# A hybrid decoder layer: the decode steps of its state-space heads in another place of the program, and dt by channel through DRAM

## The chip, the cores and the metric

One Trainium2 chip, one core. The metric is the device time of one execution in microseconds. The engines are named as in the profile: PE (TensorE: matmuls), DVE (VectorE), ACT (ScalarE), POOL (GpSimd), SP (SyncE, which here only issues transfers). Each engine works through its own instructions in an order fixed when the program is built.

## The reference

One layer for 1024 prompt positions and 8 decode rows (one new token each of 8 sequences), width 1024, all in f32:

```
proj = rmsnorm(x) @ w_in            # z (1536) | xBC (2048) | dt (24) | v (512)
xBC  = silu(causal_dwconv4(xBC));  dt = softplus(dt + bias);  a = -exp(a_log)
y    = ssd_scan(xs, dt, a, B, C, h0) + d_skip * xs      # 24 heads x 64, 4 groups of B and C, state 64, chunks of 128
y    = grouped_rmsnorm(y * silu(z)) # 4 groups of 384
x   += concat(y, pool_mixer(v)) @ w_out
x   += conv_ffn(rmsnorm(x));  out = rmsnorm(x)
```

For a decode row the scan is a single step on a state that is read from memory and written back: `h = exp(dt*a) * h0 + (dt*x) outer B`, `y = C . h + d_skip * x`. The pooling mixer subtracts the token from trailing means over 2 to 16 positions and maps each of four groups linearly. The outputs are y and all new states.

## The kernel before, in words

**Layout.** Channels lie on the 128 partitions, positions along a row: 1024 prompt columns and 8 decode columns. `win` is cut into 32 column tiles of 128: 0 to 11 are xs (12 tiles, two heads each), 12 and 13 are B and 14 and 15 are C of two halves, 16 to 27 are the gates z, 28 to 31 are v. Every f32 operand is split into a high part (an ACT copy to fp32r) and a low part (a subtraction); a product is three matmuls: high by high (L159), high by low (L160), low by high (L161), summed in PSUM in three pieces of 344 columns. Weights come in pieces of 128x512 by SP into `raw` (4 buffers, L130) and are split into `wop` (4 buffers): the high part on ACT (L140), the low part on `self.lo_eng` (L141), which is POOL for xs tiles 1 to 9 and DVE afterwards.

**Order of the program.** `startup` norms the input in three pieces (`norm`: L313 multiply, L319 high part, L329 low part, with a list `low` that delays the low parts by two multiplies) and computes tiles 12, 14 and 0. `dt_chain` turns dt to softplus, then makes running sums (`cum`, L422), their logarithms and exponentials, and writes the negated sums to DRAM (`acd`, L447). At its end it brings the decode rows' dt to a layout by channel: a transpose (L452), a copy, a masked multiply (L456), a select matmul (L461), `dtS`, and `dA = exp(-dt*exp(a_log))` (L470). `tables` chains ACT's table functions: each stands behind the one traced before it.

`ssd_phase` computes tiles 1 to 5; then tiles 13, 15, 6 to 9 with the first half's chunks between them (`ssd_tasks(0)`, taken from a queue by `between` at each piece of 344 columns); then tiles 10 and 11 with decode steps 0 to 2 between them; then gates 0 to 6 (tiles 16 to 22) with the second half's chunks, and decode steps 3 to 6 in four of these (L790). A `conv_tile` is convolved on ACT (L514) and DVE (three L516); its SiLU follows later.

**One chunk** of 128 positions has three functions. `decay` loads `mix` and `ce` from `acd`, shifts mix on DVE (L538), takes twelve exponentials of it and one of ce on ACT (L188) and multiplies ce by C on POOL (L553). `turn` transposes x and B on PE (L565, L574), copies them out (L575), masks C.B (L576), and multiplies (L578, L583). `apply` computes the chunk's state (L597, PSUM bank `pM`, of which there is one), the state's decay on POOL (L606) and sum on DVE (L610), and the output in bank `pY` (L620 from mix, L630 from ce), which L638 adds to xs.

**One decode step** (`sample_tile`, one of 12 tiles of xs) is POOL's: it loads the state (L666, 256 KB; every third tile, or at tile 7, also the rows of B and C, L662, that `sample_bc` wrote to DRAM after a transpose into `pM` and a copy), then does `dx`, `tmp = B*dx` (L671), `st = st*dA` (L672), their sum (L673), the store (L674), the product with C (L675), a tree of six additions (L680) and two small ones on xs (L681, L682). Its tags: `st`, `stt` and `bc` have one buffer each in the chunk stage; `sample_bc`'s small copy shares `stt`. Steps 7 to 11 stand in `project` beside gates 7 to 11, where the tags are shared with the pooling tiles (`v`, `mh`, `ml`, `vs`).

**A gate** (`gate_tile`) copies z out (L693), takes SiLU of all 1032 columns, multiplies the prompt columns of xs (L698) and the decode columns (L700); after every third, `group_norm` squares all 1056 columns (L710, L712, sums on POOL, L714, or on DVE for the last two groups) and `group_scale` sums over partitions by a matmul with ones (L721), takes Ln and Exp and scales prompt (L730) and decode columns (L730 again). Then come the four pooling tiles (`pool_tile`: v out of PSUM L847 and L849, pooling state by SP L843, first `memset` on POOL L842), `w_out`, and the ConvFFN, which takes the second half of the time.

The program is traced in this order, but the Tile framework places the instructions on each engine by a timeline of its own at build time: the program's order is a priority, and what is ready earlier by that timeline may go ahead. A tile whose tag has no free buffer waits until the older tile's last reader is done.

Of the kernel before, what the change touches and what calls it, by code (L numbers as in the profile page):

```python
# [10 lines left out]
F32 = mybir.dt.float32  # L11
# [59 lines left out]

M_ID, M_TRI, M_SEL, M_RM = 0, 128, 256, 384
NMAT = 384 + 12


class Kernel:
# [143 lines left out]
    def startup(self, first):  # L220
# [3 lines left out]
        with tc.tile_pool(name="start", bufs=1) as sp:  # L224
# [78 lines left out]
            def norm(c, ss, also=None):  # L303
# [6 lines left out]
                for k in range(KT):  # L310
# [10 lines left out]
                    if also is not None and k == 0:  # L321
                        with self.behind(act):
                            also()
                    while low and (len(low) > 2 or k == KT - 1):
                        j, xj = low.pop(0)
                        hi, lo = self.hn[j]
                        eng = nc.gpsimd if j == 2 or (j == 5 and c > 0) else nc.vector
                        with self.behind(prev if eng is nc.vector else None):
                            sub = eng.tensor_tensor(  # L329
                                out=lo[:, cols], in0=xj, in1=hi[:, cols].bitcast(F32), op=ALU.subtract  # L330
                            )
# [45 lines left out]
    def dt_chain(self, sp, dps):  # L377
# [34 lines left out]
        self.dt = self.const.tile([P, n9], F32, name="dt")  # L412
        nc.vector.scalar_tensor_tensor(out=self.dt, in0=t, scalar=0.0, in1=l, op0=ALU.max, op1=ALU.add)
        ea = cut(4 * n9, NH)
        self.tables(ea, self.c("alr", 0, NH), AF.Exp)
# [24 lines left out]
        for half in range(2):  # L440
# [12 lines left out]
        dts = cut(4 * n9 + NH, NB)  # L453
        nc.vector.tensor_copy(dts[:NH], tp[:NH, :NB])
        r = cut(900, XT * NB).rearrange("p (i b) -> p i b", b=NB)
        nc.vector.tensor_tensor(  # L456
            out=r[:NH], in0=self.mat[:NH, M_RM : M_RM + XT].unsqueeze(2).broadcast_to([NH, XT, NB]),
            in1=dts[:NH].unsqueeze(1).broadcast_to([NH, XT, NB]), op=ALU.mult,
        )
        tp = self.bank("pT")  # L460
        nc.tensor.matmul(  # L461
            tp[:, : XT * NB], self.mat[:NH, M_SEL : M_SEL + P], r[:NH].rearrange("h i b -> h (i b)"),
            start=True, stop=True,
        )
        self.dtS = self.const.tile([P, XT, NB], F32, name="dtS")
        nc.vector.tensor_copy(self.dtS.rearrange("p i b -> p (i b)"), tp[:, : XT * NB])
        ec = cut(1000, XT)
        self.tables(ec, self.c("alc", 0, XT), AF.Exp)
        self.dA = self.const.tile([P, XT, NB], F32, name="dA")
        nc.vector.scalar_tensor_tensor(  # L470
            out=self.dA, in0=self.dtS, scalar=-1.0, in1=ec.unsqueeze(2).broadcast_to([P, XT, NB]),
            op0=ALU.mult, op1=ALU.mult,
        )
        self.tables(self.dA, self.dA, AF.Exp)

# [177 lines left out]
    def sample_tile(self, q, i):  # L653
# [3 lines left out]
        mk = lambda s, shape: self.ph.tile(shape, F32, tag=self.tags[s][0], name=self.nm(s), bufs=self.tags[s][1])  # L657
        if i % 3 == 0 or i == 7:
            self.bc = mk("bc", [P, 2, NB, NST])
            for j in range(2):  # L660
                src = self.bcd[q : q + 1, :, j * P + g * NST : j * P + (g + 1) * NST]
                nc.gpsimd.dma_start(self.bc[:, j], src.rearrange("o b n -> (o b) n").partition_broadcast(P))  # L662
# [5 lines left out]
        tmp = mk("stt", [P, NB, NST])  # L668
        bcast = lambda a: a.unsqueeze(2).broadcast_to([P, NB, NST])
# [14 lines left out]
    def gate_tile(self, n, i, between):  # L684
# [10 lines left out]
        def gate():  # L695
            z = box[0]
            self.tables(z, z, AF.Silu)
            nc.vector.tensor_tensor(out=y[:, :SEQ], in0=y[:, :SEQ], in1=z[:, :SEQ], op=ALU.mult)  # L698
            ys = self.xs_samp(y)
            nc.vector.tensor_tensor(out=ys, in0=ys, in1=z[:, SEQ:TOK], op=ALU.mult)  # L700
            if i % 3 == 2:
                self.group_norm(i // 3)
# [4 lines left out]
    def group_norm(self, g):  # L707
        nc = self.nc
        sq = [self.short(SW, "sq") for _ in range(2)]
        nc.scalar.activation(sq[0], self.xs[3 * g], AF.Square)  # L710
        for i in range(1, 3):
            nc.scalar.activation(sq[1], self.xs[3 * g + i], AF.Square)  # L712
            eng = nc.gpsimd if g < 2 else nc.vector
# [3 lines left out]
    def group_scale(self, g, sq):  # L717
        nc = self.nc
        for j, (o, w) in enumerate(((0, 512), (512, 512), (1024, 32))):
            pb = self.bank(("pT", "pY")[j % 2])  # L720
# [3 lines left out]
        for i in range(3):  # L724
            y = self.xs[3 * g + i]
            for o, a, r in (
                (y[:, :SEQ], y[:, :SEQ], sq[1][:, :SEQ]),
                (y[:, SEQ:TOK], self.xs_samp(y), self.xs_samp(sq[1])),
            ):
                nc.vector.scalar_tensor_tensor(  # L730
                    out=o, in0=a, scalar=self.c("nw", 3 * g + i), in1=r, op0=ALU.mult, op1=ALU.mult
                )

    def project(self):

        nc, d, tc = self.nc, self.d, self.tc
        self.bcd = self.dram.tile([2, NB, 2 * P], F32, name="bcd")
        self.xs, self.bt, self.ctl = [None] * XT, {}, {}

        with ExitStack() as outer:  # L740
# [5 lines left out]
            with self.banks(g=4, pT=2, pY=1, pM=1) as self.ps, tc.tile_pool(name="mix", bufs=1) as self.ph:  # L746

                self.tags = {"bc": ("v", 2), "st": ("mh", 1), "stt": ("ml", 1), "dx": ("vs", 2)}
                for i in range(7, 12):
                    self.sample_tile(1, i)  # L750
                    self.gate_tile(16 + i, i, None)
                self.pool_groups()

    def ssd_phase(self):
# [19 lines left out]
        def ssd_tasks(q):  # L774
# [5 lines left out]
            def step(c):  # L780
# [18 lines left out]

        self.lo_eng = nc.gpsimd  # L800
        for n in range(1, 6):
            self.keep(n, self.conv_tile(n, n, None))
        ssd_tasks(0)
        credit[:] = 0.35, 0.6
        for n in (13, 15, 6, 7, 8, 9):
            self.keep(n, self.conv_tile(n, n, between))
        flush()
        self.lo_eng = nc.vector
        self.sample_bc(1)
        for i in range(3):  # L810
            queue.append(lambda i=i: sample(i))
        credit[1] = 0.7
# [698 lines left out]
def _mats():  # L1511
# [3 lines left out]
    m[:, M_TRI : M_TRI + P] = s <= t  # L1515
    m[:, M_SEL : M_SEL + P] = (s % 2) == (t // 64)
    m[:, M_RM : M_RM + XT] = (s // 2) == np.arange(XT)[None, :]
    return m
# [94 lines left out]
```

## Time and profile before

| | |
|---|---|
| median of 3 runs | 1408.72 us (1400.76 to 1411.55) |
| the profiled execution's own time | 1407.76 us |
| its span, first to last instruction | 1406.0 us |
| mean granted PE clock | 0.984 |
| chunk stage of the first half | about 117 to 220 us |
| chunk stage of the second half | about 269 to 390 us |
| gates 7 to 11 | about 397 to 465 us |
| bytes moved by DMA | 228.09 MB |

The page's first part gives each engine's busy time, share of the span and number of instructions. A row of the timeline reads: start, duration, engine, line, operation, output<-inputs, count; in brackets the idle time of that engine just before and what ended it. A row of the waits reads: who waited, for whom: us in total, times, the longest. A row of the stages reads: from:to, length, then busy us (and instructions) of PE, weight load, DVE, ACT and POOL, the granted PE clock, the share of the DMA engines and GB/s. A row of the groups reads: instruction and shape xcount | busy us, mean ns | idle before.

### The profile page before, as it was taken

Reading aid. Unit: us, or ns where it says so; the run is one execution under the profiler, and the core shown is the slowest. Engines: PE = TensorE matmul, PEld = TensorE weight load, DVE = VectorE, ACT = ScalarE, POOL = GpSimd, SP = SyncE. Lnnn points to the kernel's source line nnn. Section 1 sums busy time; section 2 is a strip of 40 time slices with the busy share of each in tenths; the row PEclk is TensorE's granted clock in tenths of the full one; section 3 lists DMA queues with packets and bytes.
Section 4 is the critical chain, followed back from the end, with each engine's and each line's share of the span. In section 5 each row is a group of like instructions: output and inputs, shape, how many; then the busy total and the mean of one; then the engine's idle time right before and its main releaser. Section 6 shows DMA issues by size and latency. Waiting matters only on the chain. (4 is left out here: it accounts for less than half of the span.)

```text
span 1406.0 us, 26779 instructions
## 1 busy us (share of the span) xinstructions
PE 1360.4 (97%) x10360; PEld 1312.9 (93%) x10360; DVE 991.2 (70%) x1453; ACT 700.6 (50%) x1408; POOL 561.5 (40%) x704
## 2 busy tenths in 40 slices
PE   8999999979999999999979999999999999999997
PEld 7799879968799999899979999999999999999997
DVE  6575898669865684844689877777776787567743
ACT  6346774546644451311456545554554465444452
POOL 4233465888668305774222212212222224214122
PEclk9999999989999999999999999999999999999999
DMA  6031235243331256675477877777777769657513
GB/s 248 1 108 38 93 118 168 81 142 116 94 104 62 74 192 209 214 253 178 152 204 148 210 205 193 187 207 183 185 187 201 196 207 328 225 185 235 180 55 121
DMA packets 117820, 228.09 MB, mean 162 GB/s; under 512 B 19884, under 2 KB 37116, under 8 KB 117692
## 3 DMA queue, kind: packets, MB, share of 16 engines
q1 hardware_dynamic: 73772, 130.21, 29.3%
q0 software_dynamic: 27056, 70.22, 19.8%
q10 hardware_dynamic: 16864, 25.95, 5.6%
q8 instruction: 81, 1.33, 0.4%
q14 instruction: 47, 0.39, 0.1%
HBM read 169.64 MB, written 45.15 MB: 153 GB/s over the span
## 5 line engine op out<-in xcount | busy, mean ns | idle before, releaser
L1118 PE MATMUL g<-op,wop 128*128 128x258 f32 x3696 | 446.9, 283 | 4.3 <-DVE op L1048 1.6
L1118 PEld LDWEIGHTS g<-op,wop 128*128 128x128 f32 x3696 | 445.3, 189 | 5.6 <-DVE op L1048 2.0
L140 ACT ACTIVATE wop<-raw 128x512 fp32r<-128x512 f32 (+1 forms) x208 | 125.9, 608 | 231.2 <-PE g L161 139.7
L1300 PE MATMUL g<-op,wop 128*128 128x258 f32 x1848 | 224.9, 283 | 1.6 <-ACT op L210 0.9
L159 PE MATMUL g<-hh,wop 128*128 128x344 f32 x696 | 226.1, 325 | 0.0
L160 PE MATMUL g<-hl,wop 128*128 128x344 f32 x696 | 225.3, 324 | 0.0
L1300 PEld LDWEIGHTS g<-op,wop 128*128 128x128 f32 x1848 | 222.5, 189 | 2.7 <-ACT op L210 1.1
L161 PE MATMUL g<-hh,wop 128*128 128x344 f32 x696 | 224.8, 323 | 0.0
L141 DVE TENSOR_TENSOR wop<-raw,wop 128x512 fp32r<-128x512 f32 (+1 forms) x186 | 159.7, 862 | 83.3 <-ACT wop L140 81.5
L140 ACT ACTIVATE wop<-s 128x512 fp32r<-128x512 f32 (+1 forms) x136 | 83.6, 620 | 137.6 <-PE g L1300 51.9
L1098 POOL DMA_DIRECT2D s<-s x44 | 37.7, 857 | 249.8 <-DVE wop L141 89.2
L159 PEld LDWEIGHTS g<-hh,wop 128*128 128x128 f32 x696 | 132.2, 190 | 1.2 <-issue 1.1
L161 PEld LDWEIGHTS g<-hh,wop 128*128 128x128 f32 x696 | 132.1, 190 | 1.2 <-issue 1.2
L160 PEld LDWEIGHTS g<-hl,wop 128*128 128x128 f32 x696 | 132.1, 190 | 0.5 <-issue 0.4
L1200 DVE SCALAR_TENSOR_TENSOR acc<-u,cst,acc 128x1048 f32<-128x1048 f32 x88 | 115.2, 1309 | 12.2 <-ACT acc L1198 10.6
L141 DVE TENSOR_TENSOR wop<-s,wop 128x512 fp32r<-128x512 f32 (+1 forms) x136 | 92.1, 682 | 36.5 <-ACT wop L140 34.1
L1178 DVE TENSOR_TENSOR u<-u,g 128x258 f32<-128x258 f32 (+2 forms) x176 | 58.0, 354 | 72.2 <-PE g L1118 67.6
L1175 ACT ACTIVATE u<-g 128x258 f32<-128x258 f32 (+2 forms) x220 | 69.6, 340 | 71.2 <-PE g L1118 71.2
L160 PE MATMUL g<-yl,wop 128*128 128x344 f32 x288 | 93.4, 325 | 3.2 <-DVE yl L211 3.2
L161 PE MATMUL g<-yh,wop 128*128 128x344 f32 x288 | 93.0, 323 | 0.0
L159 PE MATMUL g<-yh,wop 128*128 128x344 f32 x288 | 92.9, 323 | 0.0
L1270 POOL DMA_DIRECT2D g<-td x77 | 41.2, 539 | 123.1 <-DVE op L211 70.2
(276 smaller groups left out, 2333.9 us busy)
## 6 DMA issues: line engine op xcount, KB each, us to landing
s<-wup SPq DMA_DIRECT2D x88, 256.0 KB, 3.2
g<-td POOLq DMA_DIRECT2D x77, 258.0 KB, 4.5
raw<-wup SPq DMA_DIRECT2D x66, 256.0 KB, 4.1
raw<-win SPq DMA_DIRECT2D x58, 256.0 KB, 2.7
mix<-acd SPq DMA_DIRECT2D x16, 768.0 KB, 4.5
td<-acc ACTq DMA_DIRECT2D x22, 516.0 KB, 6.1
s<-wup POOLq DMA_DIRECT2D x44, 256.0 KB, 5.3
s<-s POOLq DMA_DIRECT2D x44, 256.0 KB, 3.9
```

The lines of the kernel that those rows point to most:

```text
L140: self.nc.scalar.activation(hi, raw[:, :w], AF.Copy)
L141: lo_eng.tensor_tensor(out=lo, in0=raw[:, :w], in1=hi.bitcast(F32), op=ALU.subtract)
L159: nc.tensor.matmul(ps[:, :n], wh, xh[:, sl], start=(first and k == 0), stop=False)
L160: nc.tensor.matmul(ps[:, :n], wh, xl[:, sl], start=False, stop=False)
L161: nc.tensor.matmul(ps[:, :n], wl, xh[:, sl], start=False, stop=(final and k == last))
L1098: nc.gpsimd.dma_start(t, raw[acc] if acc in raw else w[acc][j], accum_op=ALU.add)
L1118: nc.tensor.matmul(out, a, b, start=(p in OPENS and j == 1), stop=(j == 12), skip_group_check=True)
L1175: a = nc.scalar.activation(out, ps[:, s], AF.Copy, scale=-1.0 if p in ("p5", "p4") else 1.0)
L1178: nc.vector.tensor_tensor(out=out, in0=out, in1=ps[:, s], op=op)
L1200: nc.vector.scalar_tensor_tensor(out=acc, in0=u[:, k : k + FW], scalar=self.c("fw", 3 * n + k), in1=acc, op0=ALU.mult, op1=ALU.add)
L1270: self.loaded = self.nc.gpsimd.dma_start(st[:, j], self.td[i + j][ROW[p]]).ins
L1300: self.pe = nc.tensor.matmul(out, a, b, start=(s == 0 and i == 0 and j == 0), stop=(s == len(PIECES) - 1 and i == nk - 1 and j == 2),).ins
```

## The change

Seven things are changed together.

1. `dtS` and `dA` are made right behind `dt`: the decode rows' dt goes to DRAM (`dtd`, transposed by the access pattern) and back as two broadcasts over 64 partitions, all three issued by ACT. The transpose, mask and select matmul go, and two blocks of the constant `mat` with them.
2. `sample_bc(0)` and decode steps 0 to 4 stand behind conv tiles 1 to 5, step 5 behind tile 13; `sample_bc(1)` stands behind the first half's chunk 2.
3. Steps 6 to 8 stand beside gates 7 to 9, steps 9 to 11 behind gate 11. The rows of B and C (`bc`) share the tag `pf` (2 buffers); for steps 9 to 11 state and `tmp` share one tile of that tag.
4. The low parts of the weights of tiles 1 to 5 (and what is loaded ahead for them) go from POOL to DVE.
5. For gates 6 to 11, SiLU of the decode columns goes to a tile of its own (`zs`); their gate, and the group norm of groups 2 and 3, treat prompt columns alone.
6. `group_decode` gates and norms the decode columns of groups 2 and 3, behind pooling tiles 3 and 1.
7. In `norm` of the first piece, the low part is delayed by one multiply, not by two.

```diff
-                    while low and (len(low) > 2 or k == KT - 1):
+                    while low and (len(low) > min(c + 1, 2) or k == KT - 1):
...
         nc.vector.scalar_tensor_tensor(out=self.dt, in0=t, scalar=0.0, in1=l, op0=ALU.max, op1=ALU.add)
+
+        dtd = self.dram.tile([NH, NB], F32, name="dtd")
+        nc.scalar.dma_start(dtd.rearrange("h b -> b h"), self.dt[:NB, n8:n9])
+        self.dtS = self.const.tile([P, XT, NB], F32, name="dtS")
+        for g in range(2):
+            nc.scalar.dma_start(self.dtS[64 * g : 64 * g + 64], dtd[g::2].partition_broadcast(64))
+        ec = cut(1000, XT)
+        self.tables(ec, self.c("alc", 0, XT), AF.Exp)
+        self.dA = self.const.tile([P, XT, NB], F32, name="dA")
+        nc.vector.scalar_tensor_tensor(
+            out=self.dA, in0=self.dtS, scalar=-1.0, in1=ec.unsqueeze(2).broadcast_to([P, XT, NB]),
+            op0=ALU.mult, op1=ALU.mult,
+        )
+        self.tables(self.dA, self.dA, AF.Exp)
...
-        tp = self.bank("pM")
-        nc.tensor.transpose(tp[:NH, :NB], self.dt[:NB, n8:n9], self.mat[:NB, M_ID : M_ID + NB])
...
-        self.tables(self.dA, self.dA, AF.Exp)
...
-        if i % 3 == 0 or i == 7:
+        if i % 3 == 0:
...
-        st = mk("st", [P, NB, NST])
+        if self.tags["st"] is None:
+            pair = self.ph.tile([P, 2, NB, NST], F32, tag="pf", name=self.nm("st"), bufs=2)
+            st, tmp = pair[:, 0], pair[:, 1]
+        else:
+            st, tmp = mk("st", [P, NB, NST]), mk("stt", [P, NB, NST])
...
-            self.tables(z, z, AF.Silu)
+            if i < 6:
+                self.tables(z, z, AF.Silu)
+            else:
+                self.tables(z[:, :SEQ], z[:, :SEQ], AF.Silu)
+                self.tables(self.zs[:, i - 6], z[:, SEQ:TOK], AF.Silu)
...
+    def group_decode(self, g):
+
+        nc = self.nc
+        pb = self.bank("pT")
+        for i in range(3):
+            y, s = self.xs[3 * g + i], self.zs[:, 6 + i]
+            rows = y[:, SEQ:TOK]
+            nc.vector.tensor_tensor(out=rows, in0=self.xs_samp(y), in1=self.zs[:, 3 * g + i - 6], op=ALU.mult)
+            nc.vector.tensor_tensor(out=s, in0=rows, in1=rows, op=ALU.mult)
+            nc.tensor.matmul(pb[:, :NB], self.ones, s, start=(i == 0), stop=(i == 2))
+        r = self.zs[:, 9]
+        self.rsqrt(r, pb[:, :NB], 1.0 / 384.0)
+        for i in range(3):
+            rows = self.xs[3 * g + i][:, SEQ:TOK]
+            nc.vector.scalar_tensor_tensor(
+                out=rows, in0=rows, scalar=self.c("nw", 3 * g + i), in1=r, op0=ALU.mult, op1=ALU.mult
+            )
...
-                self.tags = {"bc": ("v", 2), "st": ("mh", 1), "stt": ("ml", 1), "dx": ("vs", 2)}
+                self.tags = {"bc": ("pf", 2), "st": ("mh", 1), "stt": ("ml", 1), "dx": ("vs", 2)}
                 for i in range(7, 12):
+                    if i < 10:
+                        self.sample_tile(1, i - 1)
+                    self.gate_tile(16 + i, i, None)
+                self.tags["st"] = None
+                for i in range(9, 12):
                     self.sample_tile(1, i)
-                    self.gate_tile(16 + i, i, None)
...
-                if c == -1 and q == 0:
-                    self.sample_bc(q)
-                if q == 1 and c in (0, 2, 4, 6):
-                    sample(3 + c // 2)
+                if (q, c) == (0, 2):
+                    self.sample_bc(1)
...
-        self.lo_eng = nc.gpsimd
         for n in range(1, 6):
             self.keep(n, self.conv_tile(n, n, None))
+            if n == 1:
+                self.sample_bc(0)
+            sample(n - 1)
         ssd_tasks(0)
         credit[:] = 0.35, 0.6
+        self.lo_eng = nc.gpsimd
         for n in (13, 15, 6, 7, 8, 9):
             self.keep(n, self.conv_tile(n, n, between))
+            if n == 13:
+                sample(5)
         flush()
         self.lo_eng = nc.vector
-        self.sample_bc(1)
-        for i in range(3):
-            queue.append(lambda i=i: sample(i))
...
             pf[g] = self.pool_tile(g, g == 0)
+            if g in (3, 1):
+                self.group_decode(2 if g == 3 else 3)
```

More of the change, by code (lines that the diff above doesn't have):

```diff
@@ L69 @@
 NCONST = _n
-M_ID, M_TRI, M_SEL, M_RM = 0, 128, 256, 384
-NMAT = 384 + 12
+M_ID, M_TRI = 0, 128
+NMAT = 256
 class Kernel:
@@ L449, in dt_chain @@
         )
-        tp = self.bank("pM")
-        nc.tensor.transpose(tp[:NH, :NB], self.dt[:NB, n8:n9], self.mat[:NB, M_ID : M_ID + NB])
[L453 to L473, printed above, removed]
-        self.tables(self.dA, self.dA, AF.Exp)
     def samp(self, t):
@@ L708, in group_norm @@
         nc = self.nc
-        sq = [self.short(SW, "sq") for _ in range(2)]
-        nc.scalar.activation(sq[0], self.xs[3 * g], AF.Square)
+        w = SW if g < 2 else SEQ
+        sq = [self.short(SW, "sq")[:, :w] for _ in range(2)]
+        nc.scalar.activation(sq[0], self.xs[3 * g][:, :w], AF.Square)
         for i in range(1, 3):
-            nc.scalar.activation(sq[1], self.xs[3 * g + i], AF.Square)
+            nc.scalar.activation(sq[1], self.xs[3 * g + i][:, :w], AF.Square)
             eng = nc.gpsimd if g < 2 else nc.vector
@@ L718, in group_scale @@
         nc = self.nc
-        for j, (o, w) in enumerate(((0, 512), (512, 512), (1024, 32))):
+        for j, (o, w) in enumerate(((0, 512), (512, 512), (1024, 32))[: 3 if g < 2 else 2]):
             pb = self.bank(("pT", "pY")[j % 2])
@@ L727, in group_scale @@
                 (y[:, :SEQ], y[:, :SEQ], sq[1][:, :SEQ]),
-                (y[:, SEQ:TOK], self.xs_samp(y), self.xs_samp(sq[1])),
-            ):
+                (y[:, SEQ:TOK], self.xs_samp(y), self.xs_samp(sq[1]) if g < 2 else None),
+            )[: 2 if g < 2 else 1]:
                 nc.vector.scalar_tensor_tensor(
@@ L738, in project @@
         self.xs, self.bt, self.ctl = [None] * XT, {}, {}
+        self.zs = self.const.tile([P, 10, NB], F32, name="zs")
         with ExitStack() as outer:
@@ L1515, in _mats @@
     m[:, M_TRI : M_TRI + P] = s <= t
-    m[:, M_SEL : M_SEL + P] = (s % 2) == (t // 64)
-    m[:, M_RM : M_RM + XT] = (s // 2) == np.arange(XT)[None, :]
     return m
```

6 lines of the change are left out of this document (3 added, 3 removed).

## The prediction

> **What bounds the kernel now.** The page was read first, then the waits of TensorE (PE), then busy time by stage, then engine timelines around the longest waits.
>
> ```profile
> span 1406.0 us, 26779 instructions
> PE 1360.4 (97%) x10360; PEld 1312.9 (93%) x10360; DVE 991.2 (70%) x1453; ACT 700.6 (50%) x1408; POOL 561.5 (40%) x704
> ```
> ```profile
> PE pY L630 <- POOL ce L553: 9.8, 2, 9.2
> PE pM L565 <- DVE h L610: 3.7, 4, 1.9
> PE g L160 <- DVE hl L329: 2.6, 2, 2.3
> PE pY L620 <- DVE mix L583: 2.9, 2, 2.1
> PE pT L571 <- DVE cb L576: 2.8, 1, 2.8
> ```
> ```profile
> 100.00:140.00 40.00, 40.00 (x257) 39.29 (x256) 22.88 (x24) 26.39 (x50) 15.67 (x19) 1.00 0.13 40
> 140.00:190.00 50.00, 46.80 (x401) 41.54 (x400) 44.93 (x59) 34.99 (x78) 26.56 (x21) 0.97 0.37 119
> 280.00:305.00 25.00, 15.81 (x107) 12.77 (x106) 14.11 (x26) 11.17 (x25) 18.98 (x27) 0.73 0.41 122
> 305.00:390.00 85.00, 78.69 (x627) 69.05 (x626) 76.32 (x100) 53.56 (x114) 67.27 (x60) 0.96 0.35 112
> 390.00:465.00 75.00, 75.00 (x497) 72.17 (x496) 41.50 (x48) 36.98 (x55) 57.34 (x73) 1.00 0.28 87
> 296.10:302.90 6.80, 6.80 (x43) 4.97 (x45) 2.33 (x7) 0.00 (x0) 6.15 (x11) 0.50 0.10 39
> 337.00:340.40 3.40, 3.40 (x14) 3.12 (x13) 3.40 (x2) 1.99 (x7) 2.48 (x2) 0.51 0.33 122
> 378.00:381.40 3.40, 3.39 (x21) 2.11 (x22) 3.40 (x3) 3.37 (x5) 3.17 (x2) 0.50 0.02 7
> ```
>
> PE is busy 97% of the span, so only its 45.6 idle us, and the stretches at half clock after some waits, can be won. A stage row reads: its length, then busy us (and instructions) of PE, weight load, DVE, ACT, POOL, then the granted clock. PE is idle 9.2 us in 280 to 305 and 6.3 us in 305 to 390: the second half's chunks, with decode steps on POOL beside them. The last three rows are half-clock stretches behind those waits: 6.8, 3.4 and 3.4 us at 0.50, half of each lost: 6.8 us. So this stage loses 9.2 + 6.3 + 6.8 = 22.3 us.
>
> Whether POOL's decode steps are the cause stands in three timelines, ACT, POOL, PE:
>
> ```profile
> 279.37 0.83 ACT L188 ACTIVATE ce<-ce 128x768 f32<-128x768 f32 x1
> 291.18 0.83 ACT L188 ACTIVATE ce<-ce 128x768 f32<-128x768 f32 x1
> ```
> ```profile
> 280.53 1.84 POOL L662 DMA_DIRECT2D bc<-bcd  x2
> ...
> 286.69 1.83 POOL L671 TENSOR_TENSOR stt<-bc,dx 128x512 f32<-128x512 f32 x1 [2.15 <-DMA bc<-bcd]
> ...
> 293.24 1.03 POOL L672 TENSOR_TENSOR st<-st,dA 128x512 f32<-128x512 f32 x1 [2.45 <-DMA st<-st_ssm]
> 294.24 1.79 POOL L553 TENSOR_TENSOR ce<-ce,xs 128x768 f32<-128x768 f32 x1
> ```
> ```profile
> 296.08 1.54 PE L630 MATMUL pY<-ce,h 64*64 64x128 f32 x12 [9.19 <-POOL ce L553]
> ...
> 310.40 0.87 PE L597 MATMUL pM<-xd,bT 128*64 128x384 f32 x4
> ```
>
> Chunk 1's ce left ACT at 280.2, but POOL, in order, had decode steps 2 and 3 ahead of the multiply, with waits for their transfers, and came to it at 294.24. PE had stood since 286.9. The smaller waits name DVE, yet POOL stands behind the 2.8 us one:
>
> ```profile
> 259.35 0.69 DVE L141 TENSOR_TENSOR wop<-raw,wop 128x512 fp32r<-128x512 f32 x1 [3.45 <-ACT wop L140]
> ```
> ```profile
> 330.13 5.25 DVE L141 TENSOR_TENSOR wop<-raw,wop 128x512 fp32r<-128x512 f32 x1
> 335.31 0.55 DVE L575 COPY xd<-pT 128x384 f32<-128x384 f32 x1
> ```
> ```profile
> 330.07 2.48 POOL L714 TENSOR_TENSOR sq<-sq,sq 128x1056 f32<-128x1056 f32 x1
> 332.50 1.04 POOL L671 TENSOR_TENSOR stt<-bc,dx 128x512 f32<-128x512 f32 x1
> ```
>
> The same subtraction takes 0.69 us alone and 5.25 us beside an unbroken run of POOL work; the copy that PE waits for starts behind it.
>
> **The change, part by part.**
>
> Decode steps 0 to 5 leave the chunks of the second half, 6 goes behind them. What stays there for POOL is ce, the state multiply h and the squares. I take 20 of the 22.3 us as won (bounds 12.6, the long wait with its half clock, and 22.3). What is late next: chunk 2, whose ce leaves ACT at 292.0 (second ACT row). PE began chunk 2 at 310.4, 14.3 us after the wait, 3.4 of them lost to the clock; without the wait it comes there at 286.9 + 10.9 = 297.8, later than 292.0, so the wait is not handed on at once.
>
> Where do steps 0 to 5 go? One step's price is read where POOL has little else:
>
> ```profile
> L674 POOL DMA_DIRECT2D ssm_s<-stt x5 | 3.0, 602 | 1.5 <-POOL stt L673 1.5
> L672 POOL TENSOR_TENSOR st<-st,dA 128x512 f32<-128x512 f32 x5 | 6.4, 1286 | 6.7 <-DMA st<-st_ssm 6.7
> ```
>
> Five steps ran there, one store each, for the 57.3 us of POOL in the row 390 to 465: 11.4 us of POOL each and, with the wait for st (6.7 over five) and small gaps, some 14 us from one to the next (an estimate). Their start hangs on SiLU of B and C, which today stands behind dA in ACT's order of tables:
>
> ```profile
> 109.95 0.28 ACT L188 ACTIVATE dA<-dA 128x96 f32<-128x96 f32 x1 [3.41 <-DVE dA L470]
> 110.24 1.28 ACT L181 ACT_TABLE_LOAD   x1
> 111.53 4.98 ACT L188 ACTIVATE xs<-xs 128x1056 f32<-128x1056 f32 x5
> ```
> ```profile
> 69.75 0.39 DVE L413 SCALAR_TENSOR_TENSOR dt<-dtw 128x216 f32<-128x216 f32 x1
> ```
> ```profile
> DMA to landing us min/median/max: 4.7/5.5/6.1
> ```
>
> dt is ready at 70.1. The route through DRAM is two transfers one after the other; by the bc loads (last row, 4.7 to 6.1 us) they are bounded at 12 us, so dA can be there by 82 instead of 110. SiLU follows by about 90, since the convolution's sums come first on DVE, and the B and C rows of step 0, through DRAM again, by about 102 (both estimates from these rows). The price of the route: exp of a_log, and with it the running sums and acd, now stand behind dA on ACT, up to 12 us later than now. The first chunk's POOL work was only due at 143 (row below), which covers it; without cover PE would stand up to those 12 us at the sums. Two issues on ACT also wait for the first landing, with PSUM copies of PE queued behind them; three banks cover that. I take 0.
> ```profile
> L456 DVE TENSOR_TENSOR dtw<-mat,dtw 24x96 f32<-24x96 f32 x1 | 1.3, 1337 | 0.0
> L730 DVE SCALAR_TENSOR_TENSOR xs<-xs,cst,sq 128x8 f32<-128x8 f32 x12 | 5.6, 467 | 0.0
> ```
>
> The dearest instruction of the removed select costs 1.3 us of DVE. The two decode norms put 18 eight-column instructions in place of 12: 2.8 us more of DVE at 0.47, beside the pooling tiles, whose matmuls cover it (without them, 2.8). Net 0.
>
> The lower halves of tiles 1 to 5, ten subtractions, move to DVE: 6.9 us at 0.69, in 70 us where (row 100 to 140) DVE is 57% busy. Hidden; at 5.25 each they would not be.
>
> From 102 to the first chunk's POOL work, three steps fit:
>
> ```profile
> 143.13 1.82 POOL L553 TENSOR_TENSOR ce<-ce,xs 128x768 f32<-128x768 f32 x1 [10.30 <-ACT ce L188]
> ```
>
> Three remain, 34 us of POOL, in a stage where DVE is 90% and POOL 53% busy (row 140 to 190). What a step beside chunks costs: 305 to 390 held steps 4 to 6 and lost 6.3 + 3.4 = 9.7 us, 3.2 each; over the whole stage 22.3 for five, 4.5 each. Three steps: 9.7 to 13.4, and 0 if the order leaves POOL's chunk work ahead. I take 8, under the nearest row, because the idle POOL of 100 to 140 may hold more than three. The small copy for the second half's B and C now waits for step 5 to free its buffer, holding the bank pM that the chunks use; that is within these 8.
>
> The Trainium skill's page "SBUF — State Buffer", section "Who interferes with whom", says that a DVE instruction with two SBUF inputs and a GpSimd one that reads SBUF exclude each other for the whole instruction. The 5.25 us row agrees. By it, the sum would be that of the third rival below, 1419, against 1397 by the stage rows.
>
> Startup: hl of the first tile comes ahead of the third multiply.
>
> ```profile
> 12.77 1.59 DVE L313 SCALAR_TENSOR_TENSOR x<-x,cst,rs 128x344 f32<-128x344 f32 x1
> ```
>
> So it starts 1.5 us sooner; PE's 2.3 us wait there shrinks, but hl of the next tile then follows its own multiply. I take 1 (0 to 3.2, the upper with the half clock gone: 3.4 us at 0.50).
>
> ```profile
> 16.20:19.60 3.40, 3.40 (x13) 3.25 (x13) 3.40 (x7) 2.13 (x6) 0.43 (x1) 0.50 1.06 376
> ```
>
> Late steps: beside the last gates POOL now has six steps instead of five, 11.4 to 14 us more, and steps 9 to 11 share one buffer. Queued behind: the loads of pooling state on SP wait for dx of steps 10 and 11, and the next tiles' weights stand behind them on SP; PE waits for those. Gates cover part of it. I take 2 us lost (0 to 14, one step).
>
> Sum against the profiled execution, 1407.76 us with 1406.0 of span: 1407.8 - 20 - 1 + 8 + 2 = 1396.8, say **1397**. The median of three runs was 1408.72, 1 us above it.
>
> **The rivals.**
>
> *Nothing comes back.* POOL's idle time of 100 to 140 (24 us) and of the chunk stage behind it (23 us) takes the steps, and the chunks' POOL work keeps its place: 1407.8 - 20 - 1 = 1387. For: those 47 us are most of the 68 that six steps need, and only the chunks after 190 meet the rest; against: the B and C rows may come later than 102.
>
> *The stall only changes its place.* Late steps: SP held for 12 us as steps 10 and 11 run late, PE starved as long, its half clock 3.4: 1407.8 - 21 + 8 + 12 + 3.4 = 1410. For: SP's order is fixed beforehand and both buffers' waits lie in it; against: PE has no idle time at all in 390 to 465.
>
> *DVE locked out in the first half's chunks: slower.* In 140 to 190 DVE has 5.1 us free. If each of the 34 POOL us of three steps keeps DVE out, DVE ends 29 us late there, and PE, which waits for its mix and xd, with it, plus 3.4 of clock: 1407.8 - 21 + 29 + 3.4 = 1419. It decides from 18 us of delay on. For: the 5.25 us row. Against: in 305 to 390 DVE and POOL were busy 143.6 us of 85 together, so most DVE work does run beside POOL.
>
> *It does not do what it says.* The waits stay since ACT's exps, not POOL, hold the chunks: 1407. Against: ce was ready 14 us ahead of its multiply.
>
> **How the numbers follow.** My forecast 0.40; nothing comes back 0.25; stall moved 0.14; DVE locked out 0.14; no effect 0.07. The forecast's own range is 1390 to 1404; below it the second case, which with all 22.3 and startup's 3.2 makes 1382; above it the third and the fourth: 1380 to 1419. One per cent is about what a measurement of this kernel can tell from no change; it lies at 1394.6 and 1422.8. Faster by more: nearly all of the second case and a third of mine, 0.39. Slower by more: most of the lock-out's upper half and what was not thought of, 0.11. Within: 0.50.
>
> **What would show it.** Right: no wait of PE for ce of 9 us, none for cb, and clock 1.00 through the second half's chunks; SiLU of B and C by 95; POOL's six steps between 100 and 200. Wrong: PE waits for ce, h or mix in the first half's chunks above 8 us; a wait for cum behind dA; PE waiting for wop while SP sits at the pooling state.

## The result, and the profile after

| | before | after |
|---|---|---|
| median | 1408.89 us (4 runs) | 1424.27 us (4 runs, 1422.13 to 1425.17) |
| ratio | 1 | 1.0117, 95% interval 1.0074 to 1.0159 |
| profiled execution, span | 1407.76, 1406.0 us | 1424.34, 1422.6 us |
| `cum` on PE | 74.1 us | 87.0 us |
| last copy of gate 11 | 464.5 us | 478.8 us |
| last matmul of the down projection | 1395.7 us | 1409.1 us |

The changed kernel is 1.2% slower; 1397 was forecast. The last three rows place the loss: 14 us are lost before the last gate, nothing in the second half of the time, and 3.2 more behind the last matmul. The page's first lines, then the waits of PE:

```profile
span 1422.6 us, 26777 instructions
PE 1369.8 (96%) x10365; PEld 1317.2 (93%) x10365; DVE 972.9 (68%) x1466; ACT 702.4 (49%) x1416; POOL 546.1 (38%) x692
```
```profile
PE pT L436 <- DVE dtw L431: 7.2, 1, 7.2
PE pY L609 <- DVE mix L572: 6.9, 3, 5.9
...
PE g L161 <- POOL wop L141: 2.9, 1, 2.9
...
PE pY L619 <- POOL ce L542: 2.2, 1, 2.2
PE g L159 <- ACT u L490: 2.1, 2, 1.1
PE g L160 <- DVE hl L329: 1.5, 2, 0.8
...
PE pM L586 <- DVE bcs L639: 1.0, 1, 1.0
```

The 9.2 us wait for ce is gone; new ones stand for the running sums (L436 is `cum`), for `mix`, for a lower half on POOL and for `bcs`, the small copy of `sample_bc`. The stages of the changed kernel:

```profile
70.00:100.00 30.00, 22.84 (x132) 22.37 (x131) 7.65 (x11) 10.51 (x19) 1.42 (x2) 0.83 0.09 20
...
140.00:190.00 50.00, 40.94 (x299) 37.10 (x299) 40.16 (x45) 33.00 (x75) 45.86 (x53) 0.95 0.30 98
190.00:220.00 30.00, 27.89 (x221) 24.65 (x218) 21.81 (x26) 19.19 (x46) 25.59 (x30) 0.92 0.38 124
220.00:280.00 60.00, 56.04 (x401) 48.55 (x400) 42.95 (x54) 23.26 (x53) 39.89 (x39) 0.94 0.28 89
280.00:305.00 25.00, 25.00 (x203) 23.04 (x202) 21.33 (x34) 15.48 (x27) 3.33 (x3) 1.00 0.45 147
305.00:390.00 85.00, 82.01 (x670) 69.99 (x670) 71.62 (x116) 62.75 (x145) 29.20 (x14) 1.00 0.31 101
390.00:465.00 75.00, 74.36 (x510) 69.75 (x507) 39.88 (x58) 38.66 (x60) 61.64 (x76) 1.00 0.29 88
```

and of the kernel before, two rows that the prediction did not show:

```profile
70.00:100.00 30.00, 30.00 (x194) 29.59 (x193) 21.96 (x21) 13.81 (x27) 7.96 (x6) 1.00 0.38 118
...
220.00:280.00 60.00, 60.00 (x432) 57.92 (x431) 46.26 (x54) 31.81 (x69) 43.32 (x50) 1.00 0.36 110
```

The second half's chunks (280 to 390) did what was forecast: PE idle 3.0 us instead of 15.5, clock 1.00. The time went in three other places.

**The sums, 70 to 100 us.** The chain that `dt` sets off:

```profile
69.89 0.55 ACTq L416 DMA_DIRECT2D dtd<-dt  x1
76.94 2.17 ACTq L419 DMA_DIRECT2D dtS<-dtd  x2
79.15 0.46 ACT L490 ACTIVATE u<-g 128x344 f32<-128x344 f32 x1 [9.30 <-issue]
85.01 0.26 DVE L423 SCALAR_TENSOR_TENSOR dA<-dtS,dtw 128x96 f32<-128x96 f32 x1 [15.15 <-DMA dtS<-dtd]
85.30 0.28 ACT L188 ACTIVATE dA<-dA 128x96 f32<-128x96 f32 x1 [5.17 <-DVE dA L423]
85.49 0.21 ACT L188 ACTIVATE dtw<-cst 128x24 f32<-128x24 f32 x1
87.04 1.01 PE L436 MATMUL pT<-dtw,mat 128*128 128x192 f32 x2 [7.16 <-DVE dtw L431]
```
```profile
87.04:92.42 5.38, 5.38 (x18) 5.38 (x19) 2.00 (x5) 2.48 (x5) 0.04 (x1) 0.50 0.30 95
```

and `cum` in the kernel before:

```profile
74.14 0.49 PE L422 MATMUL pT<-dtw,mat 128*128 128x192 f32 x2
```

The write of 24 by 8 numbers (768 bytes) left at 69.89; ACT could issue the loads that wait for it only at 76.94, 7.05 us later, and stood 9.3 us in all; DVE stood 15.2 us for dtS. `ea`, exp of a_log (the row at 85.49), stands behind dA in ACT's chain, and `cum` needs it: `cum` came 13 us late, PE waited 7.2 us and ran 5.4 us at half clock, which makes 9.9 us lost. The Trainium skill's page "DMA: Bandwidth & Descriptors", section "Anatomy of one DMA — SWDGE (gpsimd) path", puts the fixed cost of a transfer on GpSimd's queue at about 2 us, most of it the receipt of the write; on that queue (run 8 below) this small transposed write took 7.1 us from issue to landing, and the measurement decides.

**The first half's chunks, 140 to 280 us.** PE is idle 15.1 us instead of 4.1, and three half-clock stretches (from 168, 188 and 229 us, with 3.4, 6.1 and 6.1 us of PE's work in them, half of it lost: 7.8) replace one of 3.4 (1.7): 22.9 us lost instead of 5.8, 17.1 more. The steps came too late for the idle POOL ahead of the chunks:

```profile
105.11 1.09 ACT L188 ACTIVATE xs<-xs 128x1056 f32<-128x1056 f32 x1 [1.18 <-DVE xs L505]
...
120.57 0.41 DVE L639 COPY bcs<-pM 8x256 f32<-8x256 f32 x1
121.00 0.30 SPq L640 DMA_DIRECT2D bcd<-bcs  x1
125.33 1.89 POOL L651 DMA_DIRECT2D bc<-bcd  x2
...
130.54 1.92 POOL L663 TENSOR_TENSOR stt<-bc,dx 128x512 f32<-128x512 f32 x1 [1.45 <-DMA bc<-bcd]
```

SiLU of B and C began at 105, not by 90; the rows were asked for at 125, not there by 102. Step 0 ended at 145.5 and step 5 at 256.6, so all but the first ran beside the chunks, and there they ended 18 to 27 us apart, where 14 was the estimate. What that costs shows in the longest wait there:

```profile
159.56 1.80 DVE L527 SCALAR_TENSOR_TENSOR mix<-acl,mix 128x1536 f32<-128x1536 f32 x1
...
178.82 4.24 DVE L527 SCALAR_TENSOR_TENSOR mix<-acl,mix 128x1536 f32<-128x1536 f32 x1 [0.97 <-DMA mix<-acd]
...
184.41 4.27 DVE L572 TENSOR_TENSOR mix<-mix,cb 128x768 f32<-128x768 f32 x1
...
189.48 1.00 DVE L572 TENSOR_TENSOR mix<-mix,cb 128x768 f32<-128x768 f32 x1
```
```profile
188.73 1.12 PE L609 MATMUL pY<-mix,xd 128*64 128x128 f32 x8 [5.93 <-DVE mix L572]
```

Two DVE operations took 8.5 us instead of 2.8 beside an almost unbroken run of POOL work (products and loads of the decode steps, the chunk's h and ce): 5.7 us, about the whole wait. The page "SBUF — State Buffer" of the Trainium skill, cited in the prediction, agrees with these rows too. But meeting POOL does not always cost DVE. Of the changed kernel's 48 operations of these two kinds (16 at L527, 32 at L572), the 23 that met no POOL product took at most 1.75 and 0.95 us, and the 12 that took over a tenth longer had all met one; yet of the 13 that had POOL products beside them for nine tenths of their time, 8 took no longer.

**The end.** Behind the last matmul stands POOL's DRAIN (the group's durations are in ns, minimum, median, maximum), before and after:

```profile
L1589 POOLq DRAIN  x3: 46/93/6474, 1398.7 to 1405.7; - x3
```
```profile
L1612 POOLq DRAIN  x3: 46/93/9659, 1412.1 to 1422.3; - x3
```

3.2 us more, although the transfers of the output take no longer. These places sum to 9.9 + 17.1 + 3.2, less 19.3 in the second half's chunks and 0.8 in the startup: 10 us of the 16.6. The other 6 to 7 us lie between `cum` and the last gate; no wait or clock row names them (short waits in front of matmuls whose ends are modelled count as busy), and they stay open.

### The profile page after: what moved, and what is told of

It is laid out like the page before. It is cut to its first block, busy times and chain, and to the rows that moved or that the text cites. A ratio compares the mean times of both kernels' runs of the same rounds, so it can differ in the third digit from the quotient of the medians.

```text
span 1422.6 us, 26777 instructions
## 1 busy us (share of the span) xinstructions
PE 1369.8 (96%) x10365; PEld 1317.2 (93%) x10365; DVE 972.9 (68%) x1466; ACT 702.4 (49%) x1416; POOL 546.1 (38%) x692
## 3 DMA queue, kind: packets, MB, share of 16 engines
q0 software_dynamic: 26896, 69.69, 19.7%
## 4 chain that ended last, share of the span: by engine, by line
PE 79%; DVE 7%; POOL 4%; DMA 4%; issue 2%; ACT 1%; DVEq 0%; SPq 0%; ACTq 0%; POOLq 0%
PE g L1143 30%; PE g L1325 15%; PE g L161 9%; PE g L159 9%; PE g L160 9%; PE pY L609 1%; DVE wop L141 1%; POOL st L672 1%; PE pY L619 1%; DVE mix L572 1%; DVE x L1027 1%; POOL wop L141 1%; PE pM L586 1%; DVE xs L505 1%; DMA ds<-wdn 1%
## 5 line engine op out<-in xcount | busy, mean ns | idle before, releaser
L141 DVE TENSOR_TENSOR wop<-raw,wop 128x512 fp32r<-128x512 f32 (+1 forms) x196 | 151.7, 778 | 88.5 <-ACT wop L140 86.6
L1200 ACT ACTIVATE u<-g 128x258 f32<-128x258 f32 (+2 forms) x220 | 69.6, 341 | 69.6 <-PE g L1143 69.5
L505 DVE SCALAR_TENSOR_TENSOR xs<-u,cst,xs 128x1056 f32<-128x1056 f32 x48 | 75.5, 1597 | 20.2 <-ACT xs L503 19.8
```

What stands on the lines that cost most here:

```text
L141: lo_eng.tensor_tensor(out=lo, in0=raw[:, :w], in1=hi.bitcast(F32), op=ALU.subtract)
L505: nc.vector.scalar_tensor_tensor(out=out, in0=u[:, k : k + SW], scalar=self.c("cw", 4 * ct + k), in1=out, op0=ALU.mult, op1=ALU.add)
L1200: a = nc.scalar.activation(out, ps[:, s], AF.Copy, scale=-1.0 if p in ("p5", "p4") else 1.0)
```

## The experiments

Theory A: the way of dt through DRAM, ahead of `ea` in ACT's chain, costs some 10 us. Theory B: decode steps beside the first half's chunks cost the rest. Rivals: the copy `bcs` that holds bank `pM`, the lower halves on DVE, the later sums as the cause of both. Theory C came from the first results. Unless said, a run changes the changed kernel.

**1. The dt block behind acd.** The whole `+` block of `dtd`, `dtS`, `dA` moved, unchanged, to the end of `dt_chain`.

> The changed kernel with one move: the transfers of dt, dtS, exp of a_log by channel and dA stand behind the write of acd, at the end of dt_chain, instead of ahead of ea. Theory A (the DRAM route ahead of ea holds the running sums: PE's 7.2 us wait at cum and the half clock behind it): cum is back at about 74 us, that wait is gone, and the time falls by 8 to 10 us, to 1414 to 1416 us. Rival (the route costs whatever its place, since ACT's own issues wait for the first landing with PSUM copies queued behind them): a wait of the same kind comes back between 85 and 110 us, and the time stays at 1421 to 1425. In both the decode steps start later, by up to 12 us, which by theory B (steps beside the first half's chunks cost) takes back up to 5.

1427.93 us (ratio to before 1.0135, 1.0111 to 1.0160). `cum` came at 73.4 and the last gate 7 us sooner than in the changed kernel (471.8), yet the whole was no faster: from the last gate to `w_out` it took 60.2 us instead of 52.5. Neither theory said that; the cause is in runs 3 and 6. Three rows of ACT in this run show what the edit moved:

```profile
66.50 0.21 ACT L188 ACTIVATE dtw<-cst 128x24 f32<-128x24 f32 x1
...
69.43 0.55 ACTq L453 DMA_DIRECT2D dtd<-dt  x1
76.68 2.63 ACTq L456 DMA_DIRECT2D dtS<-dtd  x2
```

The transfers kept their time, and ACT still stood 9.6 us behind the first; but `ea` (the row at 66.50) came ahead of them, and that was enough for `cum`.

**2. `sample_bc(1)` late.**

```diff
-                if (q, c) == (0, 2):
-                    self.sample_bc(1)
...
         self.lo_eng = nc.vector
+        self.sample_bc(1)
         credit[1] = 0.7
```

> The changed kernel with sample_bc(1) back behind the first half's chunks, so that its small copy no longer waits, with bank pM held, for step 5 to give up the buffer. Theory B1 (this hold, which keeps the turn of chunk 3 until 252 us, is what gives the gain back): turns come at their old pace, chunk 3 at about 205, the waits of PE at 227 and 247 us with their half clock (some 4 us and 3.4) go, and the time falls by 7 us or more, to 1412 to 1417. Theory B2 (the steps' work on POOL and DVE beside the chunks costs, whatever the copy does): the chunks that now come earlier meet steps 3 to 5 and wait for ce and mix instead: 1421 to 1428.

1431.69 us (1.0159, 1.0130 to 1.0187). Chunk 3 turned at 206 instead of 252, but the last gate ended at 478.0, as in the changed kernel (478.8); ce now cost 7.7 us at 227. Taking the hold away won nothing: B1 is out. The 7 us more came, as in run 1, behind the last gate.

**3. Steps 3 to 5 late.**

```diff
             if n == 1:
                 self.sample_bc(0)
-            sample(n - 1)
+            if n <= 3:
+                sample(n - 1)
...
-            if n == 13:
-                sample(5)
...
         self.sample_bc(1)
+        for i in range(3, 6):
+            queue.append(lambda i=i: sample(i))
         credit[1] = 0.7
```
(on top of run 2)

> The changed kernel with only steps 0 to 2 ahead of the chunks; steps 3 to 5 and sample_bc(1) stand behind the first half's chunks, beside tiles 10 and 11. Theory B (steps 3 to 5 are what the first half's chunks lose by, 11 us of waits and 6.6 of half clock more than before): those go, and three steps at 11.4 to 14 us end at about 300, where the first ce of the second half is due: 1407 to 1413, less if nothing collides there. Rival (the first half's chunks lose by the later cum and acd, not by the steps): the waits of 180 to 250 us stay, and the time is 1420 to 1425.

1411.95 us (1.0032, 1.0011 to 1.0054). The last gate ended at 462.4, 16.4 us sooner than in the changed kernel, with the late `cum` still there: theory B, and more than its 8. Against run 2, which has the same loss behind the last gate, the medians differ by 19.7 us. Behind the last gate it lost 8 us again, and here one sees to what. DVE and POOL, then PE:

```profile
475.51 0.21 POOL L674 TENSOR_TENSOR xs<-xs,dx 128x8 f32<-128x8 f32 x1
475.75 0.17 DVE L739 TENSOR_TENSOR xs<-xs,zs 128x8 f32<-128x8 f32 x1 [6.29 <-POOL xs L674]
475.83 1.22 DVE L712 TENSOR_TENSOR sq<-sq,sq 128x1024 f32<-128x1024 f32 x1
...
477.11 2.08 PE L719 MATMUL pT<-sq,ones 128*128 128x512 f32 x2 [5.62 <-DVE sq L712]
```

A multiply of `group_decode` (L739) stands in DVE's queue ahead of the last square sum of the group norm (L712). It waits for the last decode step on POOL, and with it L712 and PE. In the changed kernel PE's own order had the ones matmul late enough to miss it (step 11 ended at 485.6, PE came to it at 487.8). That is theory C.

**4. Before, with the way through DRAM alone.** The dt block of the change, and the select route taken out, in the kernel before.

> The kernel before with part 1 of the change alone: dtS and dA right behind dt, through DRAM, ahead of ea; decode steps, halves and gates as before. Theory A: cum comes 10 to 13 us later, PE waits there and runs at half clock behind it: 8 to 10 us slower, 1417 to 1419. Rival (PE's wait there comes from the lower halves that were moved to DVE, or the chunks' slack takes it back): at most 3 us slower, 1409 to 1412.

1418.60 us (1.0072, 1.0045 to 1.0098): 9.9 us slower, and `cum` late as in the changed kernel. This is theory A.

```profile
87.17 1.01 PE L435 MATMUL pT<-dtw,mat 128*128 128x192 f32 x2 [6.88 <-DVE dtw L430]
```

**5. Lower halves of tiles 1 to 5 on POOL again.** `self.lo_eng = nc.gpsimd` back ahead of that loop.

> The changed kernel with part 4 undone: the lower halves of the weights of tiles 1 to 5 on POOL again. My step (their move to DVE is hidden): the time stays within 3 us of the changed kernel's, 1421 to 1427; the ten subtractions give POOL 10 to 15 us more ahead of step 0, so steps come a little later. Rival (the move holds DVE's sums and convolutions back, and with them SiLU of B and C and the first chunk): the first turn comes 5 us or more sooner than 142, and the time falls by 5 us or more.

1435.17 us (1.0184, 1.0140 to 1.0228), outside both expectations. The rival's sign did not come: of the first turn, the transpose of B (L554) moved from 142.2 to 122.7, but the first transposes of x (L563) moved from 122.9 to 142.8, and the turn's first copy came at 147.1 instead of 144.4. The last gate ended at 480.1, 1.3 us later. Most of the 11 us is theory C's wait again, 5.7 us here, with its half clock: 61.3 us from the last gate to `w_out` instead of 52.5. So nothing shows that the halves on DVE cost time, as predicted.

**6 and 7. `group_decode` off DVE's queue.** Its first two operations go to POOL, on top of run 1 and of run 3:

```diff
-            nc.vector.tensor_tensor(out=rows, in0=self.xs_samp(y), in1=self.zs[:, 3 * g + i - 6], op=ALU.mult)
-            nc.vector.tensor_tensor(out=s, in0=rows, in1=rows, op=ALU.mult)
+            nc.gpsimd.tensor_tensor(out=rows, in0=self.xs_samp(y), in1=self.zs[:, 3 * g + i - 6], op=ALU.mult)
+            nc.gpsimd.tensor_tensor(out=s, in0=rows, in1=rows, op=ALU.mult)
```

> The run with the dt block behind acd, and besides the first two operations of group_decode (gate and square of the eight decode columns) on POOL, behind the step that they wait for, instead of DVE. Theory C (what that run won at cum was lost again at the last gates: DVE's queue had a multiply of group_decode, which waits for POOL's step 11 until 485 us, ahead of the square sums of the last group norm, and PE stood 5.9 us for those, with half clock behind): that wait goes, last gate to first matmul of w_out takes 52 to 54 us instead of 60, and the time falls by 7 to 9 us against 1427.9, to 1418 to 1421. Rival (the late steps bound the end whatever DVE's order: w_out needs the decode columns): the wait moves to the pooling tiles or w_out, and the time stays at 1425 to 1429.

1421.67 us (1.0087, 1.0059 to 1.0115), 6.3 less than run 1; last gate to `w_out` 52.5 us.

> The run with steps 3 to 5 behind the first half's chunks, and besides the first two operations of group_decode on POOL. Theory C: its 5.6 us wait at the last gate and the half clock behind it go: 7 to 9 us less than 1412, 1403 to 1406, with the dt wait at cum still there. Rival: the wait moves on and the time stays at 1410 to 1413.

1406.55 us (0.9986, 0.9956 to 1.0015), 5.4 less than run 3; last gate to `w_out` 52.5 us, and no wait of PE there. Theory C holds; the medians moved a little less than forecast. The ten executions of this kernel lie between 1398 and 1412 us at granted clocks of 0.992 to 0.982; the profiled one took 1401.66. How far a single profile can be trusted shows here too: nothing ahead of the last gate was edited between runs 3 and 7, nor between runs 1 and 6, yet their profiles reach it at 462.4 and 456.4, and at 471.8 and 476.0. Differences of a few us between two profiles' last gates carry no weight.

**8. All repairs.** Runs 3 and 7, and the transfers of dt on POOL's queue, right behind dt, with the arithmetic of `dA` behind acd:

```diff
-        nc.scalar.dma_start(dtd.rearrange("h b -> b h"), self.dt[:NB, n8:n9])
+        nc.gpsimd.dma_start(dtd.rearrange("h b -> b h"), self.dt[:NB, n8:n9])
...
-            nc.scalar.dma_start(self.dtS[64 * g : 64 * g + 64], dtd[g::2].partition_broadcast(64))
+            nc.gpsimd.dma_start(self.dtS[64 * g : 64 * g + 64], dtd[g::2].partition_broadcast(64))
```

> All repairs: steps 0 to 2 ahead of the chunks, 3 to 5 beside tiles 10 and 11, group_decode's first operations on POOL, and the three transfers of dt issued by POOL right behind dt, while exp of a_log by channel and dA stand behind acd on ACT. If theories A, B and C add up: 1412 less 8 (C) less 9 (A) is 1395, range 1390 to 1400, below the kernel before; cum is back at 74 us. Rival (each repair only moves the loss to what waits next, as with the dt block alone): 1403 to 1410. The end behind the last matmul (13.4 us in the changed kernel, 10.3 before) shows by the way whether the number of transfers on POOL's queue sets it.

1398.59 us (0.9925, 0.9900 to 0.9950), 3.6 above the sum of the three. The repairs add up only in part: with `cum` at 73 the chunks start sooner and meet steps 1 and 2, and ACT still waits for dA, which waits for dtS, with copies that PE needs queued behind it:

```profile
85.09 0.28 ACT L188 ACTIVATE dA<-dA 128x96 f32<-128x96 f32 x1 [7.07 <-DVE dA L460]
...
92.78 0.42 PE L159 MATMUL g<-hh,wop 128*128 128x344 f32 x1 [3.59 <-ACT u L491]
```
```profile
165.54 1.56 PE L620 MATMUL pY<-ce,h 64*64 64x128 f32 x24 [6.62 <-POOL ce L543]
```

**9 and 10. Fewer steps ahead of the chunks.** As run 8, with two steps, and with one, ahead; the others of 0 to 5 beside tiles 10 and 11.

> The run with all repairs, but only steps 0 and 1 ahead of the chunks; 2 to 5 beside tiles 10 and 11. In the run with all repairs PE still waits 6.6 us for ce at 159 us and 140 to 190 runs at clock 0.86, since step 1 ends at 156 and step 2 fills POOL from 149 to 176. Theory B (each step beside the chunks costs PE): step 2 gone wins 2 to 5 us, 1394 to 1397; the wait at 159 us, which is step 1's, stays. Rival (four steps beside tiles 10 and 11 run to 305 and hold the second half's first ce instead): 1399 to 1405.

1400.60 us (0.9952, 0.9923 to 0.9981). The ce wait of the first half is gone, and one of the second half has come:

```profile
297.75 1.54 PE L620 MATMUL pY<-ce,h 64*64 64x128 f32 x12 [4.96 <-POOL ce L543]
```

> As the run with two steps ahead, with only step 0 ahead and steps 1 to 5 beside tiles 10 and 11. Theory B: the 6.6 us wait and its half clock go too, 8 to 10 us at 140 to 190, but five steps of some 12 us from 253 on end at 315, past the second half's first ce at about 290: between 1392, if they fit in front of it, and 1405, if one wait of 9 us with its half clock comes back there as in the kernel before.

1412.01 us (1.0035, 1.0013 to 1.0058), 7 above the range: besides ce (2.6 us at 302) and mix (4.6 at 319), PE waited 4.3 us at 402 for square sums behind POOL. Where the steps meet the chunks can be chosen. One step ahead is slower; two and three ahead (1400.60 and 1398.59) lie too close to be told apart.

**11. dt by the old select.** Run 8 with the kernel before's transpose, mask and select matmul at the end of `dt_chain`, nothing through DRAM.

> The run with all repairs, with the old way of dt by channel (transpose, mask, select matmul, at the end of dt_chain) in place of the way through DRAM. Theory A2 (the way through DRAM is not needed: dA comes at 85 with it, at 85 to 110 without, and step 0 waits for the rows of B and C until 122 in any case): within 3 us of 1398.6, or up to 4 us less as ACT no longer waits 7 us for dtS ahead of its PSUM copies. Rival (dA at 110 holds SiLU of B and C and with it step 0 by 10 us): 1401 to 1406.

1397.75 us (0.9928, 0.9907 to 0.9950), although its DRAIN at the end is again 9.7 us and run 8's 6.4. Its first stages:

```profile
70.00:100.00 30.00, 30.00 (x194) 29.59 (x193) 22.62 (x25) 13.85 (x25) 1.43 (x2) 1.00 0.39 118
...
140.00:190.00 50.00, 43.44 (x330) 37.39 (x329) 41.82 (x53) 32.11 (x72) 44.30 (x46) 0.90 0.31 106
```

PE never stops from 70 to 100. `dA` came at 109.4 instead of 85, and step 0's first product at 124.0 against 121.6 in run 8: it waits for the rows of B and C either way. The way through DRAM bought nothing here.

**12 and 13. The end.** Run 12 loads the rows of B and C once more at step 7 in the changed kernel, which makes 271 transfers on POOL's queue, as before, and not 269; run 13 does it in run 11.

```diff
-        if i % 3 == 0:
+        if i % 3 == 0 or i == 7:
```

> The changed kernel with the rows of B and C loaded once more, at step 7 as before, so that POOL's queue issues 271 transfers as in the kernel before and not 269. If the number of transfers on that queue sets POOL's DRAIN at the end, it takes 6.5 us again instead of 9.7, and the last matmul stands 10.3 us before the end instead of 13.4; if not, 13.4 stays. The rest within 3 us of the changed kernel, or 8 us more if the last group norm falls behind step 11 on DVE as in the other runs.

The DRAIN of run 12:

```profile
L1612 POOLq DRAIN  x3: 46/102/6476, 1417.1 to 1424.1; - x3
```

1426.22 us in its one execution: 6.5 us of DRAIN, and 3.5 us of theory C's wait with its half clock instead.

> The run with the old way of dt by channel, and besides the rows of B and C loaded once more at step 7, so that POOL issues 271 transfers again. If the count of transfers on POOL's queue is what lengthens the end, and the end adds to the rest: 3 us less than 1397.75, 1393 to 1396, with the last matmul 10.3 us before the end. If the two extra loads cost in the late steps what they save at the end: 1397 to 1399.

1395.25 us (0.9915, 0.9888 to 0.9943), 2.5 less than run 11, and the DRAIN is short:

```profile
L1628 POOLq DRAIN  x3: 46/102/6472, 1387.1 to 1394.1; - x3
```

This is the lowest median of all versions: 0.85% faster than the kernel before, 2.0% faster than the changed one by the medians. That the count of transfers on POOL's queue sets the DRAIN fits all 15 kernels (269: 9.7; 271 and 272: 6.4 to 6.5), and runs 12 and 13 changed nothing but two loads; why it is so, no run shows.

## Why the prediction was wrong, point by point

| term | forecast | measured |
|---|---|---|
| second half's chunks | -20 | -19.3 |
| startup | -1 | -0.8 |
| dt through DRAM, ahead of `ea` | 0 | +9.9 |
| lower halves on DVE | 0 | no loss found (run 5) |
| `group_decode` | 0 | 0 here; 5 to 9 in runs 1, 2, 3, 5 and 12 |
| first half's chunks | +8 | +17.1 in waits and clock; run 3 won 16.4 by moving three steps (19.7 by the medians of runs 2 and 3) |
| late steps | +2 | +0.6 |
| behind the last matmul | not seen | +3.2 |
| found in no row | - | 6 to 7 |

**Right**: the diagnosis. POOL's decode steps held the second half's ce, and without them that stage lost 3 us instead of 22.3. The marker "clock 1.00 through the second half's chunks" came true.

**The step that failed first** is the sentence on the first chunk's POOL work, "only due at 143 (row below), which covers it". The delay of the sums was put right (up to 12; 13 measured), but the cover was sought at the end user, the chunk. PE takes its instructions in order: `cum` stands in its queue between the matmuls of a tile, and PE stopped there for 7.2 us, whoever needed the sums later. The prediction had the price, "without cover PE would stand up to those 12 us at the sums", and its own marker for it, "a wait for cum behind dA"; the cover named for it was none. Run 4 measured it alone: 9.9. The other cover of the same way, three PSUM banks behind ACT's stand, held only while PE stood at `cum`: with `cum` early and dt still going through DRAM (runs 1, 6 and 8 to 10) PE waited 3.2 to 3.6 us for ACT's copies at 92 us, and in run 11, without that way, it did not.

**The step that failed second** is "From 102 to the first chunk's POOL work, three steps fit". `dA` was there at 85 (82 forecast), but SiLU waited for the convolutions until 105, not 90; 8 of these 15 us went with the late `cum`, since with `cum` at 73 (runs 1 and 8) it began at 97. The rows of B and C, given 12 us, took 25, to the first product at 130.5. One step fitted. The price of a step beside chunks was also too low: three steps, taken away in run 3, won 16.4 to 19.7 us, 5.5 to 6.6 each, where 3.2 to 4.5 had been read from the second half. The price of a step alone was a little low as well: its window cuts off the end of the fifth step (470.8), and the steps' own rows from 396 to 471 sum to 12.1 us each, not 11.4.

**The third rival**, the lock-out, is part of it (5.7 us in the longest wait); its time, 1419, was nearest to the result. Its place was right, and its amount, 29 us, was not shown. One of the two rows it came from was misread: the subtraction of 0.69 us at 259.35 did not run alone, but beside a POOL product,

```profile
259.44 1.50 POOL L672 TENSOR_TENSOR st<-st,dA 128x512 f32<-128x512 f32 x1 [1.66 <-DMA st<-st_ssm]
```

so the two rows do not show that POOL always holds DVE up; the counts above say the same.

**The small copy** was put "within these 8" and was no cost of its own (run 2). **The late steps** cost little where they were feared, on SP. What they did threaten was not named: DVE's queue, where a multiply of `group_decode` stands ahead of the last group norm. The prediction costed its 18 instructions by their duration and did not ask what was queued behind their wait. The changed kernel escaped by PE's order, which was luck; five of its variants (runs 1, 2, 3, 5 and 12) did not.

**The range**, 1380 to 1419, missed by 5 us: the 12 us bound of the way through DRAM was stated and never added to its upper end.

## What to carry to other kernels

A delay of an early result is covered only if the first in-order queue that holds its consumer has other work in front of it; look for the matmul in PE's queue, not for the last user. When a step is moved into an idle stretch, work out when its last input arrives through every transfer on its way, or the idle stretch will be over. A tiny instruction that waits for a slow engine costs what stands behind it in its queue, so put it on the engine that it waits for.

## What the runs showed of the hardware

- A transposed write of 24 by 8 numbers took 7.05 us until a load that waits for it could be issued on ACT's queue (7.4 on POOL's: 69.6 to 77.0 us in run 8); the two broadcast loads then took 5.6 to 6.9 us more there.
- POOL's DRAIN at the end took 9.66 us with 269 transfers on its queue and 6.44 to 6.48 with 271 or 272, also between runs 11 and 13, which differ in two loads on that queue and nothing else.
- A wait of 2.9 us (for the lower half on POOL, at 227 us) was followed by 6.8 us of half clock, from 229 to 236, in which PE lost 3.1 us: more than the wait itself. It is no rule: in run 7, a wait of 2.7 us that ended at 183.5 left the clock at 1.00 through 165 to 191.
